# Activation buffers that begin 32 bytes apart within 256-byte lines, in a two-layer diffusion backbone

## The chip, the core and the metric

The kernel runs on one core of a Trainium2 chip. The metric is the device time of one execution in microseconds, from the core's first to its last instruction. A core has five engines with queues of their own: TensorE (PE in the rows; its weight loads are PEld), VectorE (DVE), ScalarE (ACT), GpSimd (POOL) and SyncE (SP, which here only starts transfers). Operands lie in SBUF, where each of 128 partitions has its own row of bytes; a buffer takes the same byte range in all of them. Products are summed in PSUM.

## The reference

Two layers over 512 latent tokens and 256 context tokens of 1024 features, in float32. All matrices are read from HBM in each run.

```python
for i in range(2):
    hc = modulate(cx, norm1_gain[i], mod_c[0], mod_c[1])      # RMSNorm, scale and shift
    zc = hc @ w_in[i]                                         # the last layer: keys and values alone
    hx = modulate(x, norm1_gain[i], mod_x[0], mod_x[1])
    zx = hx @ w_in[i]                                         # 1024 -> 5376
    attn_x = window_attention_with_context(qx, kx, vx, kc, vc, attn_sink[i])
    x = x + mod_x[2] * mixer_merge(zx, attn_x, *layer)        # pool, attention, spatial gating
    x = x + mod_x[5] * swiglu(modulate(x, ...), w_ffn_in[i], w_ffn_out[i])   # 1024 -> 2 x 2816 -> 1024
    # in the first layer the context goes the same way with its own attention
return rmsnorm(x, final_gain)
```

Here `mixer_merge` is `(sum over three branches of sigmoid(gate) * (y_branch @ w_br)) @ w_out`.

## The kernel before, in words

The stream of tokens is kept feature-major: features in the partitions, tokens along the row. `X` holds the residual. A large product takes a 128x128 block of a weight as the stationary operand and 512 columns (latents, `x` in a name) or 256 columns (context, `c`) of an activation tile as the moving one.

Every float32 product is made as three float32r products. `split_unit` (L272, L273) splits a weight into a high part `wh` and a low part `wl`; `split_act` (L318, L319) does the same with activations, into H and L. `gemm_step` then issues, per 128 features, wh with H (L290), wl with H (L291) and wh with L (L292). All of the gate, branch, output, query, key, value and FFN products go through it: 3 x 3112 instructions.

What stands where in SBUF: pools give out buffers of one size in turn, and the pools stand one behind the other:

- `cst`: constants, `X`, and the keys `KK` (moving operand of the scores, L505 and L511). The two tiles of `KK` begin 64 bytes into a 256-byte line.
- `rawp` (4 buffers of 4096 bytes) takes the loads of weights, and `hlp` (6 of 4096 bytes) their high and low parts. All ten begin 96 bytes into a line.
- `act` (11 buffers of 8192 bytes): high and low activations, queries, gate sums, the FFN's hidden tiles `fa`, the loaded tokens and the first modulation weights. 8192 is 32 x 256, so all eleven begin at the same place, 96 bytes into a line. A product's moving operand is a piece of such a buffer; the pieces are 1024 or 2048 bytes long and begin at multiples of 1024 bytes from the buffer's start.
- `tmp` (8 buffers of 2112 bytes), `att`, `macp` and `sml` follow. Since 2112 is 8 x 256 + 64, the buffers of `tmp` begin at 96, 160, 224 and 32 in turn.

Two lines carry this in the code:

```python
act = ctx.enter_context(tc.tile_pool(name="act", bufs=11))       # L56
hold = act.tile([P, 2 if two else 1, 2, TT], F32R, tag="S8", name=f"fa{l}{j}")   # one of its users, in ffn
```

The order of the instructions on every engine is the order in which the program is written; `Filler` mixes the vector work, a step at a time, with the large products. Nothing in that depends on an address.

Of the kernel before, what the change touches and what calls it, by code (L numbers as in the profile page):

```python
# [18 lines left out]
P = 128  # L19
# [16 lines left out]
class Stream:  # L36
    """Columns [t0, t0 + T) of the feature-major residual: the context or the latents."""

# [10 lines left out]
def hybrid_dit_kernel(ctx, tc, I, out):  # L49
# [5 lines left out]
    hlp = ctx.enter_context(tc.tile_pool(name="hlp", bufs=3))  # L55
    act = ctx.enter_context(tc.tile_pool(name="act", bufs=11))  # L56
    tmp = ctx.enter_context(tc.tile_pool(name="tmp", bufs=8))
# [17 lines left out]

# [1 line left out]
    ident = cst.tile([P, P], F32, name="ident")  # L77
# [14 lines left out]

    # rows of 128 features each, transposed to one column per row
    rowsA = t2("rowsA", P)[:48, :]
# [49 lines left out]
    def to_features(s):  # L144
        """The stream's residual to feature-major, and its tokens' sums of squares."""
        for b in range(s.t0 // P, s.t0 // P + s.NB):
            junk = act.tile([P, D], F32, tag="S8", name=f"junk{b}")
            S.activation(junk, xin[b], AF.Square, accum_out=ssx[:, b:b + 1])
            for k4 in range(2):
                ps = pmain(f"ps_xt{b}_{k4}")  # L150
                for k in range(4):
                    T_.transpose(ps[:, k * P:(k + 1) * P], xin[b][:, (k4 * 4 + k) * P:(k4 * 4 + k + 1) * P], ident)
                x = X[:, k4 * 4:k4 * 4 + 4, b * P:(b + 1) * P]
                if s is SC and k4:
                    S.activation(x, ps.rearrange("p (k t) -> p k t", k=4), AF.Copy)
                else:
                    V.tensor_copy(x, ps.rearrange("p (k t) -> p k t", k=4))
                yield

# [1 line left out]
    modv, A1, A2 = {}, {}, {}  # L161
# [10 lines left out]
    def take_mod(l, t0, n, ps, nv):  # L172
        """Rows of 32 features each to columns: tiles t0 .. t0 + n of the layer's modulation vectors."""
        mT = t2(f"mT{l}{t0}", n * 32)
        V.transpose(mT, ps)
        V.tensor_tensor(modv[l][:, t0:t0 + n, 0:nv], mT.rearrange("p (t c) -> p t c", c=32)[:, :, 0:nv],
                        colsB[:, l * 48 + t0:l * 48 + t0 + n].unsqueeze(2).to_broadcast([P, n, nv]), ALU.add)
        for dst, o, rg in ((A1[l], 8, R_N1), (A2[l], 32, R_N2)):
            a, b = max(o, t0), min(o + 8, t0 + n)
            if a < b:  # L180
                V.scalar_tensor_tensor(dst[:, a - o:b - o, 0:nv], modv[l][:, a:b, 0:nv], 1.0,
                                       colsA[:, rg + l * 8 + a - o:rg + l * 8 + b - o].unsqueeze(2).to_broadcast([P, b - a, nv]),
                                       ALU.add, ALU.mult)

    def mod_part(ps, h):
        """A quarter of the first layer's first shift and scale, on the tensor engine: loads, then two k-tiles at each step."""
        src = I["w_mod"][0, :, 0:2 * D].rearrange("(k p) (s n) -> p k s n", p=P, s=2)[:, :, :, h * 256:(h + 1) * 256]
# [16 lines left out]
    def mod_steps(l, u0, u1, stride=1):  # L204
        """The others, 512 at a time: weighted rows added up on the vector engines, then over the partitions."""
        for u in range(u0, u1):
# [35 lines left out]
    class Filler:  # L242
        """Work that is interleaved, a step at a time, with the large products."""

# [21 lines left out]

# [1 line left out]
    def split_unit(raw_ap, kt, n, nm, eng=None):  # L268
        """float32r high part and exact low part of a [P, kt, n] block of weights."""
        wh = hlp.tile([P, kt, n], F32R, tag="WH", name=f"wh_{nm}")  # L270
        wl = hlp.tile([P, kt, n], F32R, tag="WL", name=f"wl_{nm}")
        S.activation(wh, raw_ap, AF.Copy)  # L272
        (eng or V).tensor_tensor(wl, raw_ap, wh.bitcast(F32), ALU.subtract)  # L273
        return wh, wl

    def units(src, kt, nm, engs=()):
        """src [kt*P, n] -> per n-tile (wh, wl) as [P, kt, 128] views, loaded 4 KB a partition at a time."""
        n = src.shape[1]
# [18 lines left out]
    def gemms(pw, kt, H, L):  # L297
        """Products of several feature tiles with the same activations, side by side."""
        for k in range(kt):
            for ps, (wh, wl) in pw:  # L300
                gemm_step(ps, wh[:, k, :], wl[:, k, :], H[k], L[k], k == 0, k == kt - 1)

    def pair_tiles(n, T, nm):
        """n feature tiles of T columns, as high and low parts."""
        per = 2048 // T
# [17 lines left out]

# [1 line left out]
    def rstd(ss_ap, nb, nm, div):  # L325
# [6 lines left out]
    def token_ss(s, acc, nm):  # L332
        """Sums over the features of the squares that the tiles of acc hold."""
        ps = pmain(f"ps_ss_{nm}")
# [5 lines left out]
    def modulated(s, ss, A, Sh, nm, out, every=1, keep=False, HL=None):  # L340
        """Normed and modulated stream, split: the sums, the tokens' factors along the columns, the products."""
        rs = rstd(ss(), s.NB, nm, D)
# [30 lines left out]

# [1 line left out]
    KK = [cst.tile([P, 2, NT], F32R, name=f"KK{g}") for g in range(2)]  # L375
# [42 lines left out]
    def queries(s, l, H, L, rot, us, ts):  # L418
        """Rotated queries of the head pairs ts: a head's high parts in its half of the partitions, its low parts in the other."""
        Q = act.tile([P, len(ts), 2, s.T], F32R, tag="S8", name=f"Q{l}{s.name}{ts[0]}")  # L420
# [18 lines left out]
    def attention(s, l, H, L, rot, YH, YL, then=None):  # L439
        """A head pair and block of queries at each step, in a pipeline of three stages."""  # L440
        us = units(I["w_in"][l][:, OFF_Q:OFF_K], KT, f"q{l}{s.name}")
# [11 lines left out]
        def advance(w):  # L453
            """Transposes of the pair before the last and sums of the one before that; then new scores."""
            done.append(None)
# [33 lines left out]
    def score(s, l, w, Q):  # L489
        """Softmax of a head pair's scores, queries in the partitions."""  # L490
        t, b = w
# [34 lines left out]
    def turn(s, st):  # L526
        """The pair's weights with the keys in the partitions."""
        w, blocks, prs, nm = st
# [30 lines left out]
    def first_tiles(parts, e):  # L559
        """The context's first six feature tiles by quarters of the features: sv's four and two of u.  # L560

        A quarter of the modulation vectors is loaded and summed during the products of the one before."""
        cols = ((OFF_SV, 512), (OFF_U, 256))
# [112 lines left out]
    def pooling(s, l, H, L, YH, YL):  # L676
        """A pool group at each step."""
        nm0 = f"{l}{s.name}"
# [154 lines left out]
    def ffn(streams, l, hs, finish, starts=(), mods=(), parts=None, ahead=None, turn=None):  # L833
        """The up and down halves are a tile apart; starts are steps of what the last stream waits for."""
        fo = I["w_ffn_out"][l]
# [37 lines left out]
        def half(s, w, j, up, more=(), by=None):  # L873
            """Gate or up products of one stream, and of further tiles side by side."""
            pw = [(pmain(f"pf{'gu'[u]}{l}{s.name}{jj}")[:, :s.T], ww, jj, u) for ww, jj, u in ((w, j, up), *more)]
# [66 lines left out]

# [1 line left out]
    hs = {}  # L944
# [70 lines left out]
    def last_tiles(one, acc):  # L1015
        """The last products by token halves: a half is normed during the other's."""
        hs["x"] = pair_tiles(KT, SEQ, "n2x1")
# [18 lines left out]
    def first_halves(pw, H, L):  # L1036
        """The first products by token halves: the second half is normed during the first's."""
        for i in range(2):
# [17 lines left out]
    def turn(i):  # L1056
        """Residual rows to token-major, and the last gate's vector along the columns."""
        if i == 0:
# [12 lines left out]
    def finish1(c0, m, A):  # L1071
        """The last products with the tokens in the partitions; a block of tokens is normed and stored during the next."""
        ws = []
# [52 lines left out]
def _shape_constants():  # L1126
    """Rotation tables by grid position and the pools' edge factors: by shapes alone."""
    import numpy as np
# [36 lines left out]
```

## Time and profile before

| | |
|---|---|
| time, median of 2 runs | 2089.8 us (2088.78 to 2090.81) |
| profiled execution, span | 2093.8 us (no other time of it is given) |
| mean granted TensorE clock | 0.988 of full |
| TensorE busy | 2024.5 us, 97% of the span, 11615 matmuls |
| VectorE, ScalarE, GpSimd busy | 55%, 36%, 20% |
| DMA | 233.46 MB, 112 GB/s over the span |

Busy times come from one execution under the profiler. A matmul's duration holds its way through the array and overlaps the next one's, so the pace of a stream of matmuls is read from one start to the next, not from the duration.

### The profile page before, as it was taken

How to read it: one execution, taken by the hardware profiler on the slowest of the kernel's cores; microseconds unless marked ns; L12 is line 12 of the kernel's file. 1: busy time of each engine (PE TensorE's matmuls, PEld its weight loads, DVE VectorE, ACT ScalarE, POOL GpSimd, SP SyncE). 2: the span in 40 equal slices, each digit the busy share in tenths (PEclk: the TensorE clock that was granted, in tenths of full speed). 3: DMA queues.
4: the chain of work that ended last, by engine and by line, in shares of the span. 5: the costliest groups of instructions: out<-in, count | busy, mean ns of one | idle time of the engine just before them, and what ended most of it. 6: DMA issues, size and time to landing. Idle time of an engine off the chain costs nothing.

```text
span 2093.8 us, 28850 instructions
## 1 busy us (share of the span) xinstructions
PE 2024.5 (97%) x11615; PEld 1715.0 (82%) x11615; DVE 1149.6 (55%) x1765; ACT 744.4 (36%) x1231; POOL 426.7 (20%) x358
## 2 busy tenths in 40 slices
PE   7998999999899999999999999999999999999998
PEld 6988988777677888888888888787778788888887
DVE  4878638675666653434334335765756664344335
ACT  3655434344333422121313124443422333222223
POOL 4426302023664411000102013301111130000000
PEclk9999999999999999999999999999999999999999
DMA  9755633231544232222323223423336643333331
GB/s 294 207 165 153 202 101 101 63 104 51 159 153 131 81 91 73 88 81 71 91 61 101 71 71 89 109 61 90 88 102 211 178 132 91 100 95 97 101 92 59
DMA packets 326181, 233.46 MB, mean 112 GB/s; under 512 B 7648, under 2 KB 299664, under 8 KB 326048
## 3 DMA queue, kind: packets, MB, share of 16 engines
q1 hardware_dynamic: 322528, 226.78, 36.1%
q0 software_dynamic: 3280, 4.76, 1.1%
q8 instruction: 91, 1.49, 0.3%
q14 instruction: 42, 0.34, 0.0%
q10 hardware_dynamic: 240, 0.08, 0.0%
HBM read 225.30 MB, written 2.10 MB: 109 GB/s over the span
## 4 chain that ended last, share of the span: by engine, by line
PE 81%; DVE 10%; DMA 3%; issue 2%; ACT 2%; POOL 2%; ACTq 0%; SPq 0%; POOLq 0%; DVEq 0%
PE pg1x L290 2%; PE pg1x L291 2%; PE pg1x L292 2%; PE pfg0x L292 2%; PE pfg0x L291 2%; PE pfg0x L290 2%; PE pfg1x L292 2%; PE pfo0x L290 2%; PE pfo0x L291 2%; PE pfu1x L291 2%; PE pfo0x L292 2%; PE pfu1x L292 2%; PE pfu1x L290 2%; PE pfg1x L290 2%; PE pfg1x L291 2%
## 5 line engine op out<-in xcount | busy, mean ns | idle before, releaser
L220 POOL TENSOR_TENSOR mac<-mac,mq 128x512 f32<-128x512 f32 x84 | 124.4, 1481 | 296.9 <-ACT mq L219 293.0
L273 DVE TENSOR_TENSOR wl_fu<-raw_fu,wh_fu 128x1024 fp32r<-128x1024 f32 x44 | 63.6, 1446 | 153.9 <-ACT wh_fu L272 153.8
L222 DVE SCALAR_TENSOR_TENSOR mac<-wm,scv,mac 128x512 f32<-128x512 f32 x140 | 131.0, 936 | 13.4 <-DMA wm<-in_w_mod_dram 10.6
L272 ACT ACTIVATE wh_fg<-raw_fg 128x1024 fp32r<-128x1024 f32 x44 | 46.6, 1059 | 181.1 <-PE pfo0x L292 65.7
L273 DVE TENSOR_TENSOR wl_fo<-raw_fo,wh_fo 128x1024 fp32r<-128x1024 f32 x42 | 54.7, 1303 | 69.3 <-ACT wh_fo L272 69.3
L272 ACT ACTIVATE wh_fo<-raw_fo 128x1024 fp32r<-128x1024 f32 x42 | 44.4, 1058 | 122.4 <-issue 120.2
L291 PE MATMUL pg0x<-n1x0h,wl_g0x 128*128 128x512 f32 x192 | 77.2, 402 | 8.9 <-DVE wl_g0x L273 8.9
L290 PE MATMUL pg0x<-n1x0h,wh_g0x 128*128 128x512 f32 x192 | 77.1, 402 | 1.5 <-ACT wh_g0x L272 1.5
L290 PE MATMUL pg1x<-n1x1h,wh_g1x 128*128 128x512 f32 x192 | 76.4, 398 | 0.0
L292 PE MATMUL pg0x<-n1x0l,wh_g0x 128*128 128x512 f32 x192 | 76.4, 398 | 0.0
L291 PE MATMUL pg1x<-n1x1h,wl_g1x 128*128 128x512 f32 x192 | 75.8, 395 | 0.0
L292 PE MATMUL pg1x<-n1x1l,wh_g1x 128*128 128x512 f32 x192 | 75.8, 395 | 0.0
L329 POOL TENSOR_TENSOR rs_fin<-v_fin,half_neg 128x1 f32<-128x1 f32 x4 | 2.9, 721 | 355.3 <-DVE v_fin L327 355.3
L290 PE MATMUL pfg1x<-n2x1h,wh_fg 128*128 128x512 f32 (+1 forms) x184 | 70.5, 383 | 0.8 <-ACT n2x1h L359 0.8
L854 DVE SCALAR_TENSOR_TENSOR X<-pfo0x,modv,X 128x512 f32<-128x512 f32 x48 | 36.0, 750 | 64.0 <-PE pfo0x L292 64.0
L292 PE MATMUL pfg1x<-n2x1l,wh_fg 128*128 128x512 f32 (+1 forms) x184 | 70.5, 383 | 0.5 <-POOL n2x1l L360 0.3
L290 PE MATMUL pfu1x<-n2x1h,wh_fu 128*128 128x512 f32 (+1 forms) x184 | 70.0, 380 | 0.0
L291 PE MATMUL pfu1x<-n2x1h,wl_fu 128*128 128x512 f32 (+1 forms) x184 | 70.0, 380 | 0.0
L291 PE MATMUL pfg1x<-n2x1h,wl_fg 128*128 128x512 f32 (+1 forms) x184 | 69.9, 380 | 0.0
L292 PE MATMUL pfu1x<-n2x1l,wh_fu 128*128 128x512 f32 (+1 forms) x184 | 69.9, 380 | 0.0
L290 PE MATMUL pfo0x<-fa,wh_fo 128*128 128x512 f32 x176 | 69.0, 392 | 0.0
L291 PE MATMUL pfo0x<-fa,wl_fo 128*128 128x512 f32 x176 | 69.0, 392 | 0.0
(708 smaller groups left out, 6540.1 us busy)
## 6 DMA issues: line engine op xcount, KB each, us to landing
wm<-in_w_mod_dram SPq DMA_DIRECT2D x96, 512.0 KB, 4.0
raw_fg<-in_w_ffn_in_dram SPq DMA_DIRECT2D x44, 512.0 KB, 3.9
raw_fu<-in_w_ffn_in_dram SPq DMA_DIRECT2D x44, 512.0 KB, 3.8
raw_fo<-in_w_ffn_out_dram SPq DMA_DIRECT2D x42, 512.0 KB, 3.4
raw_g0c<-in_w_in_dram SPq DMA_DIRECT2D x24, 512.0 KB, 3.9
raw_g0x<-in_w_in_dram SPq DMA_DIRECT2D x24, 512.0 KB, 4.2
raw_g1x<-in_w_in_dram SPq DMA_DIRECT2D x24, 512.0 KB, 3.9
raw_wo0c<-in_w_out_dram SPq DMA_DIRECT2D x8, 512.0 KB, 4.0
```

Of the source, the lines that this page charges most:

```text
L220: G.tensor_tensor(a, a, q, ALU.add)
L222: V.scalar_tensor_tensor(a, raw[:, k, :], sck, a, ALU.mult, ALU.add)
L272: S.activation(wh, raw_ap, AF.Copy)
L273: (eng or V).tensor_tensor(wl, raw_ap, wh.bitcast(F32), ALU.subtract)
L290: T_.matmul(ps, wh, H, start=first, stop=False)
L291: T_.matmul(ps, wl, H, start=False, stop=False)
L292: T_.matmul(ps, wh, L, start=False, stop=last)
L329: G.tensor_tensor(rs, v, half_neg[:, :nb], ALU.pow)
L854: V.scalar_tensor_tensor(x, ps, modv[l][:, 40 + n, s.r:s.r + 1], x, ALU.mult, ALU.add)
```

## The change

The buffers of `act` grow from 8192 to 8224 bytes (2056 float32 numbers), and each tile uses the first bytes of its buffer as before. 8224 is 32 x 257, so buffer number b of the eleven begins at 96 + 32b, counted within 256 bytes: 96, 128, 160, 192, 224, 0, 32, 64, 96, 128, 160. The pools behind `act` move back by 11 x 32 = 352 bytes; those ahead of it (`cst`, `rawp`, `hlp`) stay. A class with a method `tile` stands in for the pool. Docstrings and comments are dropped as well. On each engine the same instructions stand in the same order with the same waits as before, and each tile has the buffer number it had.

```diff
-    act = ctx.enter_context(tc.tile_pool(name="act", bufs=11))
+    actp = ctx.enter_context(tc.tile_pool(name="act", bufs=11))
+
+    class Staggered:
+        @staticmethod
+        def tile(shape, dt, tag, name):
+            n = math.prod(shape[1:])
+            t = actp.tile([P, 2048 + 8], dt, tag=tag, name=name)[:, :n]
+            if len(shape) == 2:
+                return t
+            d = "abc"[:len(shape) - 1]
+            return t.rearrange(f"p ({' '.join(d)}) -> p {' '.join(d)}", **dict(zip(d[:-1], shape[1:-1])))
+
+    act = Staggered
```

By the places of its buffers, the program's 9336 products of L290 to L292 have moving operands that begin here:

| bytes into a 256-byte line | 0 | 32 | 64 | 96 | 128 | 160 | 192 | 224 |
|---|---|---|---|---|---|---|---|---|
| before, 512 columns | 0 | 0 | 0 | 5976 | 0 | 0 | 0 | 0 |
| before, 256 columns | 0 | 0 | 0 | 3360 | 0 | 0 | 0 | 0 |
| now, 512 columns | 856 | 296 | 864 | 1136 | 708 | 1184 | 260 | 672 |
| now, 256 columns | 16 | 176 | 224 | 168 | 296 | 1176 | 488 | 816 |

## Rows read from the trace of the kernel before

**Rows 1.** The page: span, and busy time of each engine.

```profile
span 2093.8 us, 28850 instructions
PE 2024.5 (97%) x11615; PEld 1715.0 (82%) x11615; DVE 1149.6 (55%) x1765; ACT 744.4 (36%) x1231; POOL 426.7 (20%) x358
```

**Rows 2.** The page: the chain that ended last, shares by engine.

```profile
PE 81%; DVE 10%; DMA 3%; issue 2%; ACT 2%; POOL 2%; ACTq 0%; SPq 0%; POOLq 0%; DVEq 0%
```

**Rows 3.** L290 over the span: busy us of its matmuls, then of their weight loads.

```profile
0.00:2093.80 2093.80, 1109.12 (x3112) 592.85 (x3112) 0.99 0.38 112
```

**Rows 4.** Timeline, TensorE, second half of an FFN block: start us, duration us, what.

```profile
854.43 0.28 PE L290 MATMUL pfo0c<-fa,wh_fo 128*128 128x256 f32 x1
...
855.39 0.28 PE L292 MATMUL pfo0c<-fa,wh_fo 128*128 128x256 f32 x1
855.51 0.40 PE L290 MATMUL pfo0x<-fa,wh_fo 128*128 128x512 f32 x1
855.74 0.40 PE L291 MATMUL pfo0x<-fa,wl_fo 128*128 128x512 f32 x1
855.98 0.39 PE L292 MATMUL pfo0x<-fa,wh_fo 128*128 128x512 f32 x1
...
856.67 0.39 PE L292 MATMUL pfo0x<-fa,wh_fo 128*128 128x512 f32 x1
...
858.26 0.28 PE L290 MATMUL pfo0c<-fa,wh_fo 128*128 128x256 f32 x1
```

**Rows 5.** Two stretches: busy us of PE, PEld, DVE, ACT, POOL, then granted clock.

```profile
562.70:565.70 3.00, 3.00 (x9) 2.32 (x8) 0.00 (x0) 0.00 (x0) 2.92 (x3) 0.50 0.78 237
856.60:858.30 1.70, 1.70 (x10) 1.38 (x9) 1.25 (x2) 0.00 (x0) 0.00 (x0) 1.00 0.00 0
```

**Rows 6.** Timeline, TensorE, in the first of these stretches.

```profile
563.12 0.63 PE L290 MATMUL pg0x<-n1x0h,wh_g0x 128*128 128x512 f32 x1
...
565.68 0.63 PE L290 MATMUL pg0x<-n1x0h,wh_g0x 128*128 128x512 f32 x1
```

**Rows 7.** Timeline, TensorE: scores, whose moving operand is KK.

```profile
81.98 0.28 PE L292 MATMUL pg0c<-n1c0l,wh_g0c 128*128 128x256 f32 x1
82.10 0.64 PE L511 MATMUL s0c<-KK,Q0c 128*128 128x256 f32 x4
82.57 0.28 PE L290 MATMUL pg0c<-n1c0h,wh_g0c 128*128 128x256 f32 x1
```

**Rows 8.** Timeline, TensorE: transposes, whose stationary operand is pr (96) or X (224).

```profile
97.96 0.60 PE L536 MATMUL pt0c<-ident,pr0c 128*128 128x128 f32 x4
2072.93 1.91 PE L1067 MATMUL ps_yt<-ident,X 128*128 128x128 f32 x16
```

**Rows 9.** Lines with durations, min/median/max in ns: operands in tmp's buffers.

```profile
L886 DVE TENSOR_TENSOR sg1x<-sg1x,pfu1x x22: 686/689/690, 1733.0 to 2073.1; 128x512 f32<-128x512 f32 x22
L883 ACT ACTIVATE sg1x<-pfg1x x22: 597/600/601, 1732.3 to 2064.5; 128x512 f32<-128x512 f32 x22
```

**Rows 10.** Groups of TensorE by line: busy us, mean ns of one.

```profile
L290 PE MATMUL pg0x<-n1x0h,wh_g0x 128*128 128x512 f32 x192 | 77.1, 402 | 1.5 <-ACT wh_g0x L272 1.5
L290 PE MATMUL pg1x<-n1x1h,wh_g1x 128*128 128x512 f32 x192 | 76.4, 398 | 0.0
L290 PE MATMUL pfu0x<-n2x0h,wh_fu 128*128 128x512 f32 x176 | 68.5, 389 | 0.0
```

**Rows 11.** DMA issues that write to or read from act's buffers: KB each, us to landing.

```profile
xin_c<-in_ctx_dram SPq DMA_DIRECT2D x1, 1024.0 KB, 4.9
Q0x<-ql0x POOLq DMA_DIRECT2D x8, 128.0 KB, 2.4
out_dram<-yt SPq DMA_DIRECT2D x4, 512.0 KB, 2.7
```

## The prediction

> **What bounds the kernel now.** I read the page's busy times first: TensorE works 97% of a span of 2093.8 us, and no other engine over 55% [rows 1]. The chain of waits agrees: 81% of what ended last is TensorE, 10% VectorE [rows 2]. The change alters no instruction, order or wait; it alters only where eleven buffers begin. So the question is one of duration: does any instruction take a different time when its operand begins elsewhere, and does it lie on TensorE's stream?
>
> Next I read the pace of that stream. Within a run of FFN products the start column goes from 854.43 to 855.51 over nine products of 256 columns: 0.120 us each. It goes from 856.67 to 858.26 over seven products of 512 columns: 0.227 us each [rows 4], at the full granted clock, 2.4 GHz [rows 5]. One column per cycle would be 256 / 2.4 = 106.7 ns and 512 / 2.4 = 213.3 ns. Both widths thus carry the **same excess of about 13.3 ns per product**. At the half level, 1.2 GHz [rows 5], the starts go from 563.12 to 565.68 over six products [rows 6]: 427 ns, which is 512 / 1.2 with no excess. The excess is therefore not so many cycles of the array; it looks like a fixed piece of time in fetching operands that a slower array hides.
>
> In the products of L290 to L292 (3 x 3112 [rows 3]) the excess adds up to 9336 x 13.3 ns = 124.5 us, 6% of the span. All of them read a moving operand that begins 96 bytes into a line. **This is the only sum of note that the change could touch**, and 13.3 ns is also the time in which 32 float32 columns, 128 bytes, stream in: the excess can be a fixed start of each product, or one more 128-byte step because 96 is not a multiple of 128. The rows of before contain no product that begins at 0 or 128, so they don't decide it.
>
> **The change part by part.**
>
> *Moving operands of the 9336 products.* The nearest row with another start is the scores: KK begins at 64. Four products of 256 columns follow a steady stream of the same width, and their starts go from 82.10 to 82.57: 117.5 ns each against 120 [rows 7]. So moving the start by 32 bytes was worth at most 2.5 ns there, and the excess stayed at 10.8 of 13.3. The four are few, and starts shift by a few ns where streams of different kinds meet: the first products behind a change of width take 0.23 and 0.24 us instead of 0.227 [rows 4]. I read the 2.5 ns as that. My value is 0 ns per product, by the nearest row; the ends are -13.3 ns (all of the excess gone) and +13.3 ns (one more such piece).
>
> *Stationary operands.* wh and wl stay at 96. Queries (288 score products) and the last 48 products have their stationary operand in `act`; if each gained or lost 13.3 ns that would be 336 x 13.3 = 4.5 us. Transposes show stationary operands at two places: four of pr (96) last 0.60 us together and sixteen of X (224) 1.91 us [rows 8]. Taking off one full duration of about 0.28 us, that is 0.32 / 3 = 107 ns and 1.63 / 15 = 109 ns: the same. I take 0.
>
> *VectorE, ScalarE, GpSimd.* They read and write `act`, and `tmp` moves by 352 bytes. The buffers of `tmp` already begin at four different places, and the 22 additions of L886 that go round them last 686 to 690 ns, the 22 activations of L883 597 to 601 ns [rows 9]. A start that differs by 32 bytes or a multiple changes at most 4 ns here. Few of these are on the chain (14% for the three engines [rows 2]), and I take 0.
>
> *Contention between engines.* If TensorE's reads collided with the others' accesses, products beside busy engines would be slower. The slowest large group, pg0x, has a mean of 402 ns against 389 in the undisturbed pfu0x; pg1x has 398 [rows 10]. Over three lines of 192 that is at most 13 x 576 + 9 x 576 ns = 12.7 us, waits and changes of stream included. This is the whole of what neighbours could cost now, so it bounds a gain at -12.7 us, and by the same size a loss. I take 0.
>
> *Transfers.* Loads of weights go to `rawp`, which stays. Into and out of `act` go the tokens, the first modulation weights, the queries' low parts and the result; such transfers land in 2.4 to 4.9 us [rows 11]. They began off a 256-byte line before and mostly do now. If each row of 4096 bytes took one 256-byte piece more or less than its 16, the last store would move by 2.7 / 16 = 0.2 us and the first load by 4.9 / 16 = 0.3 us. I take 0.
>
> The sum is 0: 2093.8 us for the profiled execution. That execution is 4.0 us above the median of the runs shown, so in their terms 2089.8 us.
>
> **A rule beside the row.** The Trainium skill, in "TensorE: Matmul & The Clock Gate", section "Back-to-back issue gap", gives a full-clock gap of N / 2.4 + 2.5 ns, 215.8 ns for 512 columns. This trace shows 227 [rows 4], so 10.8 ns per product are unexplained by it; were they all due to the buffers' places and gone, 9336 x 10.8 ns = 101 us would go, to 1989 us. The skill's "SBUF — State Buffer", section "Specifications", speaks against this: it names 16-byte lines, and every start here is a multiple of 32, which by that rule costs the same anywhere. No run here shows the size of a line.
>
> **The rivals.**
>
> 1. *Only multiples of 128 are free.* The excess is a seventeenth (ninth) 128-byte step. Then the products from buffers 1, 5 and 9 lose it: 856 + 708 = 1564 of 512 columns x 13.3 ns = 20.9 us, and 16 + 296 = 312 of 256 columns, where the 109 ns pace of the weight loads [rows 8] stops them at a gain of 11 ns: 3.4 us. Together -24 us, 2065 us, faster by 1.2%. For it speaks the exact size of the excess, and KK at 64 keeping most of it. If it falls smoothly instead by the 2.5 ns per 32 bytes of rows 7 within 128 bytes, the table's counts give a mean change of -3.7 ns (512) and -3.2 ns (256), -33 us, 2057 us.
>
> 2. *The gain is large.* Either multiples of 64 are free (2688 x 13.3 + 1024 x 11 ns = 47 us, 2043 us), or the excess comes from both operands beginning at the same place, 96, which now holds for only 1136 + 168 products: 4840 x 13.3 + 3192 x 11 ns = 99 us, 1990 us. Against both stand the scores: KK begins at 64 and its stationary Q at 96, and 10.8 ns of excess are left [rows 7].
>
> 3. *Slower: the upper half of a line costs one more step.* If a fetch works in lines of 256 bytes in halves, a moving operand that begins at 160, 192 or 224 takes a further 13.3 ns. That is 2116 + 2480 = 4596 products, +61 us, 2151 us, slower by 2.9%. It decides (over 2%, 42 us) from 9.1 ns per such product. No product of before begins in an upper half, so no moving operand excludes it; against it speak X at 224 as a stationary operand, which loads at the pace of pr [rows 8], and the other engines' indifference [rows 9]. A milder form has the excess grow by the 2.5 ns per 32 bytes of rows 7 over the whole line: the mean start goes from 96 to 109 (512) and 160 (256), +1.05 x 5976 + 5.0 x 3360 ns = +23 us, 2113 us.
>
> 4. *The change doesn't do what it says.* The sizes leave no room for this: the pool steps by 8224 bytes, a multiple of 32, and nothing else in it is shared with another tile. It would give the forecast's time in any case.
>
> **How the numbers follow.** The forecast, no effect of the place, has 0.59; rival 1 has 0.16, rival 2 0.10, rival 3 0.09, its milder form 0.06. The likeliest time is 2089.8 us; contention and stationary reads alone would leave it within 2073 to 2107. The range reaches to rival 1's smooth end and to the mild loss, 2056 to 2114 us, and holds 0.59 + 0.16 + 0.06 = 0.81. A difference of 2%, 42 us, is about what a measurement of this kernel can tell from no change. Faster by more is rival 2, 0.10; slower by more is rival 3, 0.09; the rest, 0.81, lies within.
>
> **What would show it.** In the changed kernel the start-to-start pace of steady runs settles it: 0.227 and 0.120 us in every run of FFN products proves the forecast, whatever buffer `fa`, n2x0h or n1x1h lies in. Rival 1 would show some runs at 0.213 to 0.216 and the rest at 0.227; since L290 and L291 read the high part and L292 the low one, a run could alternate between two paces. Rival 2 shows the fast pace in half or more of the runs, rival 3 a pace of 0.240 (512) and 0.133 (256) in buffers 2, 3, 4 and 10. L886 and L883 should stay at 689 and 600 ns. I am wrong if any steady run has a pace that differs from before by more than 2 ns.

## The result, and the profile after

| | before | after |
|---|---|---|
| time, median of 2 runs | 2089.8 us (2088.78 to 2090.81) | 2106.93 us (2106.62 to 2107.23) |
| ratio to before, 95% interval | | 1.008 (1.0051 to 1.011) |
| profiled execution: span, mean granted clock | 2093.8 us, 0.988 | 2104.4 us, 0.992 |

The change costs 17.1 us, 0.8%. That lies within 2% and within the range of the forecast, but it is not the forecast "no effect": the interval excludes a ratio of 1.

The page of the changed kernel: span, busy times, and the shares of the chain that ended last.

```profile
span 2104.4 us, 28850 instructions
PE 2033.8 (97%) x11615; PEld 1702.9 (81%) x11615; DVE 1148.0 (55%) x1765; ACT 744.0 (35%) x1231; POOL 429.4 (20%) x358
...
PE 82%; DVE 9%; DMA 3%; issue 2%; ACT 2%; POOL 1%; ACTq 0%; POOLq 0%; SPq 0%; DVEq 0%
```

Beside [rows 1, 2] TensorE's matmuls are busy for 9.3 us longer; the chain's shares agree to a point, and no new wait stands in it. Next, a stretch near the end in which TensorE never idles and no context is left, so that nearly all products have 512 columns: first before, then after (columns as in [rows 5]).

```profile
1800.00:2000.00 200.00, 200.00 (x884) 165.58 (x884) 77.68 (x85) 51.00 (x62) 0.00 (x0) 1.00 0.33 98
```

```profile
1800.00:2000.00 200.00, 200.00 (x866) 162.22 (x865) 77.33 (x84) 50.26 (x60) 0.00 (x0) 1.00 0.32 95
```

In the same 200 us at the full clock TensorE finishes 866 products instead of 884: 230.9 ns each instead of 226.2. The timeline of the changed kernel shows the pace itself (start us, duration us, what); lines 304 to 306 are L290 to L292 of before.

```profile
564.61 0.63 PE L304 MATMUL pg0x<-n1x0h,wh_g0x 128*128 128x512 f32 x1
...
565.89 0.63 PE L304 MATMUL pg0x<-n1x0h,wh_g0x 128*128 128x512 f32 x1
...
857.27 0.40 PE L304 MATMUL pfo0x<-fa,wh_fo 128*128 128x512 f32 x1
...
858.45 0.39 PE L306 MATMUL pfo0x<-fa,wh_fo 128*128 128x512 f32 x1
...
860.07 0.28 PE L304 MATMUL pfo0c<-fa,wh_fo 128*128 128x256 f32 x1
...
1006.17 0.28 PE L304 MATMUL pfu0c<-n2c0h,wh_fu 128*128 128x256 f32 x1
...
1008.98 0.39 PE L304 MATMUL pfg0x<-n2x0h,wh_fg 128*128 128x512 f32 x1
```

Twelve products of 512 columns take 2.80 us, 233 ns each. Twelve such products of before (from 855.51 to 858.26 in [rows 4]) take 2.75 us, 229 ns each. The last seven of each twelve (from 858.45 here, from 856.67 there) take 231 ns against 227. Twenty-four products of 256 columns take 2.81 us, 117 ns each, against 120. So the wide ones became slower and the narrow ones faster. At the half clock three products take 1.28 us, 427 ns, as in [rows 6]. Two of the runs below agree (426.7 ns at distance 32, 426.0 at 160): there the place does nothing.

Here and below, a mean pace is taken over all products that run at the full clock and are followed by one of the same width without a wait (some 5,700 of the 5976 and 3,100 of the 3360). It is 227.44 and 119.68 ns before, 231.45 and 117.88 ns after. 5976 x 4.01 - 3360 x 1.80 ns = **+17.9 us, as much as the whole loss**. The profiled spans differ by only 10.6 us because the execution of after met less of the half clock. Span times mean granted clock, as an estimate of the span at the full clock throughout, is 2067.9 us before and 2088.6 us after (mean clocks 0.98766 and 0.99249), 20.7 us apart.

### The profile page after: what moved, and what is told of

It is laid out like the page before. It is cut to its first block, busy times and chain, and to the rows that moved or that the text cites. A ratio compares the mean times of both kernels' runs of the same rounds, so it can differ in the third digit from the quotient of the medians.

```text
span 2104.4 us, 28850 instructions
## 1 busy us (share of the span) xinstructions
PE 2033.8 (97%) x11615; PEld 1702.9 (81%) x11615; DVE 1148.0 (55%) x1765; ACT 744.0 (35%) x1231; POOL 429.4 (20%) x358
## 3 DMA queue, kind: packets, MB, share of 16 engines
q1 hardware_dynamic: 322528, 226.78, 35.9%
## 4 chain that ended last, share of the span: by engine, by line
PE 82%; DVE 9%; DMA 3%; issue 2%; ACT 2%; POOL 1%; ACTq 0%; POOLq 0%; SPq 0%; DVEq 0%
PE pg1x L304 2%; PE pg1x L305 2%; PE pg1x L306 2%; PE pfg0x L306 2%; PE pfg1x L306 2%; PE pfg0x L305 2%; PE pfo0x L306 2%; PE pfu1x L305 2%; PE pfu1x L306 2%; PE pfo0x L305 2%; PE pfo0x L304 2%; PE pfg0x L304 2%; PE pfu1x L304 2%; PE pfg1x L305 2%; PE pfg1x L304 2%
## 5 line engine op out<-in xcount | busy, mean ns | idle before, releaser
L236 DVE SCALAR_TENSOR_TENSOR mac<-wm,scv,mac 128x512 f32<-128x512 f32 x140 | 129.3, 923 | 13.3 <-DMA wm<-in_w_mod_dram 10.7
L306 PE MATMUL pfg0x<-n2x0l,wh_fg 128*128 128x512 f32 x176 | 69.2, 393 | 0.3 <-POOL n2x0l L374 0.3
```

The costliest lines, as they stand in the source:

```text
L236: V.scalar_tensor_tensor(a, raw[:, k, :], sck, a, ALU.mult, ALU.add)
L306: T_.matmul(ps, wh, L, start=False, stop=last)
```

## The experiments

Three theories of why a moving operand's place changes the pace: **A**, its distance from the place of the stationary operand (wh or wl), both counted within 256 bytes, decides; **B**, jumps in place from one moving operand to the next cost time; **C**, its own place within a line decides (rivals 1 and 3 of the prediction).

### All buffers of `act` moved alike

The size stays 8192, so that no two moving operands differ in place, and a pad ahead of the pool moves all eleven buffers. With 8 numbers (32 bytes):

```diff
     hlp = ctx.enter_context(tc.tile_pool(name="hlp", bufs=3))
+    pad = ctx.enter_context(tc.tile_pool(name="pad", bufs=1))
+    V.memset(pad.tile([P, 8], F32, name="pad"), 0.0)
     act = ctx.enter_context(tc.tile_pool(name="act", bufs=11))
```

The others have 16, 24, 32, 40, 48, 56 and 64 numbers. `hlp` stays, so the distance from stationary to moving operand is the size of the pad. Expected, in the order in which they ran, for 32, 64 and 128 bytes:

> All eleven activation buffers begin at 128 instead of 96 (8192 bytes apart, as before); the weights' high and low parts stay at 96. Theory A (the place of the moving operand against the stationary one's, here 32 bytes apart, sets the pace): the steady paces leave 0.2267 and 0.120 us everywhere; if they go to the changed kernel's means of about 0.2315 and 0.118, the time rises by 5976 x 4.8 - 3360 x 2 ns = 22 us, to 2112 us. Theory B (a cost only where one product's moving operand begins elsewhere than the one's before): no change, 2090 us, 0.2267 and 0.120. Theory C (the absolute place, multiples of 128 free): 0.2133 in all runs, about 2090 - 117 = 1973 us.

> As the run by 32, with all activation buffers at 160, 64 bytes from the weights' 96. Theory A: paces of their own, neither those of before nor necessarily those of the shift by 32; a change of 10 us or more either way. Theory B: 2090 us, 0.2267 and 0.120. Theory C: 160 is 32 past a multiple of 128, so the excess stays: 2090 us.

> As the run by 32, with all activation buffers at 224, half a 256-byte line from the weights' 96. Theory A: the largest change of the three if the two reads meet in a period of 256 bytes, none if the period is 128 or less (2090 us then). Theory B: 2090 us. Theory C with the upper half costing more: 0.240 and 0.133 us, 2090 + 124 = 2214 us; with multiples of 128 alone: 2090 us.

Then for 96, 160, 192, 224 and, in a third group, 256 bytes:

> All activation buffers 96 bytes behind the weights' place (at 192). The first four runs left Theory A alone: the place against the weights sets the pace (0: 227.4 and 119.7 ns; 32: 233.3 and 116.9; 64: 229.1 and 116.7; 128: 232.9 and 118.8). Theory A1 (even multiples of 64 are cheap, odd ones of 32 dear, 128 the exception): as by 32, about 233 and 117 ns, 2114 us. Theory A2 (no pattern in 32s): anything from 227 to 235.

> All activation buffers 160 bytes behind the weights' place (at 0, a full 256-byte line's start). Theory A with a period of 128 bytes: as by 32, 233.3 and 116.9 ns, 2114 us; but the run by 128 differs from the one at 0, so a period of 256 is likelier. Theory C once more (the start of a 256-byte line is free): 0.2133 us, 1970 us; not expected after the run with the weights shifted too.

> All activation buffers 192 bytes behind the weights' place (at 32). Theory A with the cost even in the distance (192 is 64 ahead in a line of 256): as by 64, 229.1 and 116.7 ns, 2092 us. If it is not even, another value from 227 to 235 ns.

> All activation buffers 224 bytes behind, which is 32 ahead, of the weights' place (at 64). Theory A, even in the distance: as by 32, 233.3 and 116.9 ns, 2114 us. With these eight the changed kernel's time can be summed: its 512-column products by place against the weights 0, 32, ... 224 are 1136, 708, 1184, 260, 672, 856, 296, 864, its 256-column ones 168, 296, 1176, 488, 816, 16, 176, 224. If the places alone matter, the counts times these runs' paces give its 17 us; if switching between places costs too (Theory B), the sum falls short of it.

> All activation buffers 256 bytes further on, at 96 again. Theory A with a period of 256 bytes: as before, 227.4 and 119.7 ns, 2091 us. A longer period (512 or more): an eighth value of 229 to 234 ns for 512 columns, 2100 to 2120 us.

Measured (the fourth column is what the two paces make of 5976 and 3360 products, the fifth is against before on the same chip):

| distance, bytes | 512 columns, ns | 256 columns, ns | sum, us | measured, us | ratio, 95% interval |
|---|---|---|---|---|---|
| 0 (before) | 227.44 | 119.68 | | | |
| 32 | 233.30 | 116.95 | +25.8 | +22.5 | 1.0113 (1.0096 to 1.0129) |
| 64 | 229.07 | 116.65 | -0.4 | +0.6 | 1.001 (1.000 to 1.002) |
| 96 | 233.35 | 119.87 | +36.0 | +28.5 | 1.0145 (1.0128 to 1.0161) |
| 128 | 232.85 | 118.80 | +29.4 | +24.6 | 1.0123 (1.0107 to 1.0138) |
| 160 | 234.19 | 117.96 | +34.6 | +32.0 | 1.0156 (1.0141 to 1.0171) |
| 192 | 233.21 | 114.72 | +17.8 | +16.7 | 1.0089 (1.007 to 1.0108) |
| 224 | 233.25 | 118.46 | +30.6 | +25.0 | 1.0126 (1.0109 to 1.0143) |
| 256 | 227.45 | 119.69 | +0.1 | +1.0 | 1.0008 (0.9998 to 1.0017) |

The stretch from 1800 to 2000 us of distances 32, 64, 160 and 256, in this order:

```profile
1800.00:2000.00 200.00, 200.00 (x859) 160.92 (x858) 76.83 (x84) 49.74 (x60) 0.00 (x0) 1.00 0.31 94
```

```profile
1800.00:2000.00 200.00, 200.00 (x876) 164.09 (x875) 77.47 (x85) 50.27 (x60) 0.00 (x0) 1.00 0.32 96
```

```profile
1800.00:2000.00 200.00, 200.00 (x855) 160.80 (x854) 76.45 (x83) 49.18 (x59) 0.00 (x0) 1.00 0.31 93
```

```profile
1800.00:2000.00 200.00, 200.00 (x884) 165.62 (x883) 78.95 (x86) 51.84 (x62) 0.00 (x0) 1.00 0.33 98
```

859, 876, 855 and again 884 products: the pace comes back after 256 bytes. A period of 128 bytes is excluded by distance 128, which has 232.85 ns. Distance 64 shows that the time alone is a poor witness: its wide products lose 1.63 ns each, its narrow ones gain 3.03 ns, and the two cancel to +0.6 us. My narrower guesses within A failed: a change of 10 us at 64, one value for all odd multiples of 32 (256 columns take 116.95 ns at 32, 119.87 at 96), and a cost that is even in the distance (192 isn't like 64, and 224 is like 32 for 512 columns alone).

Since there are no jumps in these runs, B isn't needed for the effect. It adds nothing on average either: if each of the change's products ran at the mean pace of its distance (place minus 96, with the counts of the table in the section on the change), the means would be 231.42 and 117.84 ns; 231.45 and 117.88 were measured. Multiples of 128 aren't free: distance 160 begins at 0 of a line and is the slowest. The sums overstate most losses by a few us (7.5 at the most). Products at the half clock don't pay the slower pace; I take it that products that wait don't either, which no run shows by itself.

### The weights moved

With the pad of 8 numbers ahead of `rawp`, weights and activations both go from 96 to 128 (distance 0, another place). With 56 numbers ahead of `hlp` and 8 ahead of `act`, the activations are back at 96 and the weights lie at 64 (distance 32, the old place of the moving operand).

```diff
     cst = ctx.enter_context(tc.tile_pool(name="cst", bufs=1))
+    pad = ctx.enter_context(tc.tile_pool(name="pad", bufs=1))
+    V.memset(pad.tile([P, 8], F32, name="pad"), 0.0)
     rawp = ctx.enter_context(tc.tile_pool(name="rawp", bufs=4))
```

```diff
+    padh = ctx.enter_context(tc.tile_pool(name="padh", bufs=1))
+    V.memset(padh.tile([P, 56], F32, name="padh"), 0.0)
     hlp = ctx.enter_context(tc.tile_pool(name="hlp", bufs=3))
+    pada = ctx.enter_context(tc.tile_pool(name="pada", bufs=1))
+    V.memset(pada.tile([P, 8], F32, name="pada"), 0.0)
     act = ctx.enter_context(tc.tile_pool(name="act", bufs=11))
```

> Weights' loads, their high and low parts and the activation buffers all begin at 128 instead of 96: the place against each other is as before, the absolute place is not. Theory A: 2090 us, paces 0.2267 and 0.120. Theory B: 2090 us as well. Theory C (multiples of 128 free): about 1973 us, or whatever the run by 32 of the activations alone gives.

> The activation buffers stay where they are before (96); the high and low parts of the weights move to 64, so the moving operand is 32 behind the stationary one. Theory A (the two reads of TensorE, moving and stationary): as the run that moved the activations by 32 instead, 233.3 and 116.9 ns, about 2114 us. If the partner of the activations is another buffer (the loads at 96, keys, constants), or the partner is what other engines write: 2091 us.

The same stretch, first with both at 128, then with the weights alone at 64:

```profile
1800.00:2000.00 200.00, 200.00 (x884) 165.58 (x883) 79.89 (x87) 51.84 (x62) 0.00 (x0) 1.00 0.33 97
```

```profile
1800.00:2000.00 200.00, 200.00 (x859) 160.64 (x858) 76.10 (x83) 50.20 (x60) 0.00 (x0) 1.00 0.32 95
```

Both at 128: 2089.01 us, ratio 0.9992 (0.9982 to 1.0002), paces 227.40 and 119.65 ns, as before. Weights alone at 64: 2115.7 us, ratio 1.0126 (1.0109 to 1.0142), paces 233.29 and 116.94 ns, those of distance 32 within a hundredth. The moving operands lie where they lay before, and yet every product has the other pace. **This settles A against C**: it is the distance between the two operands.

### A layout by width

Distance 0 has the best mean for 512 columns, 192 for 256 columns. Two kernels give each width its own. In the first, the weights of context products keep their place and all others move by 192 bytes, as `act` does; `fa` has its context piece at 192 as well. FFN gate and up products share their weights between the streams and stay at 0. A few constants were merged to make room.

```diff
+    def halves_of(shape, nm):
+        o = 0 if "c" in nm or "first" in nm else 48
...
+        th = hlp.tile([P, 1088], F32R, tag="WH", name=f"wh_{nm}")
...
+        return [t[:, o:o + n].rearrange("p (k n) -> p k n", k=shape[1]) for t in (th, tl)]
```

> The place by width: 512-column products keep 0 bytes between their operands (227.4 ns), and 2064 of the 256-column ones get 192 (the weights' parts of the context's mixer begin 64 bytes past the activations' place, the context's part of the FFN's hidden tile 192 past it; the other 1296 stay at 0). Some small constants share space to make room. Theory A: 2064 x (119.7 - 114.7) ns = 10.2 us less, ratio 0.995. Theory B (switching between places costs): the hidden tiles alternate between places from product to product, and part of the gain is lost; ratio 0.996 or more.

Measured 2089.68 us, ratio 0.9994 (0.9984 to 1.0004): no gain that can be told. The paces did change: 2064 context products are at distance 192 and take 115.62 ns (8.4 us less), and the latents keep 227.3. The mean granted clock was 0.9883 over its eleven runs and 0.9904 over the twenty of before beside them; span times clock fell by 5.1 us (2068.0 to 2062.9, means), and the lower clock took 0.0021 x 2088 = 4.4 us back. Whether the layout or chance lowered the clock stays open, and so does what became of the rest of the 8.4 us.

The second moves only the FFN's context operands, all 1584, to distance 192:

```diff
+        if nm == "n2c0":
+            last = att.tile([P, 1280], F32R, tag="pT", bufs=1, name=f"{nm}last")
...
+                HL.append([t[:, 48 + i * T:48 + (i + 1) * T] for i in range(7)] + [last[:, 48 + x * T:48 + (x + 1) * T]])
...
-            o, a = 0, {}
+            o, a = 0 if len(streams) == 1 else 48, {}
```

> Only the context's tiles in the first layer's FFN are moved: their normed tiles and their part of the hidden tiles begin 192 bytes past the weights' place (1584 products of 256 columns); all else stays at 0. There TensorE waited only about 2 us on these products before, so a gain has no wait to turn into, unlike the context's mixer in the run by width. Theory A by the runs' paces: 1056 gate and up products x (119.9 - 114.0) ns = 6.2 us, and 528 output products, which change place every 12, x (119.3 - 117.5) ns = 1 us: -7 us, ratio 0.9966. If the gain is only moved into waits again, or into slower latents behind each change of place: ratio 0.999 to 1.000.

Measured **2085.6 us, ratio 0.997 (0.9958 to 0.9981)**, 5.6 us less than before and the fastest of all. The moved products give less than was hoped for: they take 117.26 ns, not the 114.0 that the same groups (gate, up and output of the context) had in the run with all at 192, so 1584 x 2.42 ns = 3.8 us.

The latents gave something too, although their own distance stays 0. The twelve output products that took 2.75 us in [rows 4] take 2.72 us behind context products at 192:

```profile
846.76 0.39 PE L290 MATMUL pfo0x<-fa,wh_fo 128*128 128x512 f32 x1
...
849.48 0.28 PE L290 MATMUL pfo0c<-fa,wh_fo 128*128 128x256 f32 x1
```

In the mean pfo0x went from 229.04 to 226.78 ns and pfg0x, which also follows the context, from 227.75 to 226.80; 528 products of each make 1.7 us. Together the paces give 5.5 us. Span times clock fell by 3.7 us only, and the mean granted clock was 0.9906 against 0.9894, which may be chance; how the 5.6 us divide between pace and clock isn't settled.

Why 117 and not 114? The gate and up products of one block (24 each) show it. Before, distance 0:

```profile
1003.72 0.28 PE L290 MATMUL pfu0c<-n2c0h,wh_fu 128*128 128x256 f32 x1
...
1006.60 0.40 PE L290 MATMUL pfg0x<-n2x0h,wh_fg 128*128 128x512 f32 x1
```

All at 192:

```profile
1002.57 0.28 PE L292 MATMUL pfu0c<-n2c0h,wh_fu 128*128 128x256 f32 x1
...
1005.29 0.39 PE L292 MATMUL pfg0x<-n2x0h,wh_fg 128*128 128x512 f32 x1
```

Only the FFN's context at 192, at two times:

```profile
828.44 0.51 PE L230 MATMUL ps_mod<-mac,pick 128*32 128x128 f32 x12
828.88 0.38 PE L290 MATMUL pfg0c<-n2c0h,wh_fg 128*128 128x256 f32 x1
...
829.46 0.28 PE L291 MATMUL pfg0c<-n2c0h,wl_fg 128*128 128x256 f32 x1
...
831.73 0.28 PE L290 MATMUL pfu0c<-n2c0h,wh_fu 128*128 128x256 f32 x1
...
834.45 0.39 PE L290 MATMUL pfg0x<-n2x0h,wh_fg 128*128 128x512 f32 x1
...
994.89 0.28 PE L290 MATMUL pfg0c<-n2c0h,wh_fg 128*128 128x256 f32 x1
...
997.72 0.28 PE L290 MATMUL pfu0c<-n2c0h,wh_fu 128*128 128x256 f32 x1
...
1000.55 0.39 PE L290 MATMUL pfg0x<-n2x0h,wh_fg 128*128 128x512 f32 x1
```

The 24 up products (pfu0c) take 2.88 us before (120 ns each), 2.72 with all at 192 (113), and in the last kernel 2.72 once and 2.83 (118) the other time, from the same tiles and at the same distance. So distance 192 has **two steady paces**, and once settled, each of these streams kept its own to the end. In the last kernel all 17 context gate streams that follow directly on latents' FFN products (distance 0) run at 118 ns. The three that follow `ps_mod` settle at 113 to 114 after their first four products: above, the other 20 take 2.27 us, from 829.46 to 831.73. With all at 192, 16 of the 17 that follow such latents (now at 192 too) run at 113 to 114, but the first of them at 118. So what stands ahead mostly goes with the pace that a stream has; that it alone decides isn't shown, and the first stream speaks against it. No theory foresaw this, and it is why the moved products gave 3.8 us here instead of the 9.0 us (1584 x 5.7 ns) that 114.0 ns would have given.

## Why the prediction was wrong, point by point

- **What bounds the kernel**: right. TensorE's stream sets the end, order and waits didn't change, and the pace of L290 to L292 accounts for the loss. (The 4.0 us between the profiled span and the median mix two measures: in the execution of after, the time is 2.2 us longer than the span.)
- **Moving operands of the 9336 products: the failed step.** I took 0 "by the nearest row", KK's 117.5 ns against 120 [rows 7], and read the 2.5 ns as starts that shift between streams. They fit the effect: KK lies 32 bytes ahead of Q (distance 224), where the full run has 118.46 ns. The row was also of the wrong width. It had 256 columns, on which most shifts gain; the 512 columns, which are 64% of the products and carry all of the loss, were never seen at a second distance. A term whose ends are ±13.3 ns and whose one witness is of another width should have kept most of the chance open. Measured: +4.01 and -1.80 ns.
- **The common excess of 13.3 ns**: it is not a fixed start of each product. Only at distance 0 is it nearly one value (227 or 226 ns for 86% of the 512s, 120 for 86% of the 256s); elsewhere 512 columns cost 229.07 to 234.19 ns in the mean. That it vanishes at the half clock was right.
- **Stationary operands**: their own place costs nothing, as taken (both at 128: 2089.01 us). Their place against the moving operand is the effect, and the sum had no term for that; only rival 2 named it.
- **Other engines, contention, transfers**: 0, as taken. Of the changed kernel:

```profile
L900 DVE TENSOR_TENSOR sg1x<-sg1x,pfu1x x22: 686/687/690, 1736.5 to 2083.7; 128x512 f32<-128x512 f32 x22
L897 ACT ACTIVATE sg1x<-pfg1x x22: 597/599/601, 1735.9 to 2075.0; 128x512 f32<-128x512 f32 x22
```

  These are L886 and L883 of [rows 9], within 2 ns in the median.
- **Rival 1** (multiples of 128 are free) and **rival 3** (upper half of a line): wrong, place alone decides nothing. Rival 3's mild form came nearest in time (2113 us), by a mechanism that isn't there; that the measured time lies within the range, whose upper end is this form's, is luck. **Rival 2's** second form named the right pair, both operands' places against each other, with the sign reversed: for 512 columns equal places are the best case, not the worst. I judged it by KK again, and rival 2 as a whole had 0.10. **Rival 4**: the buffers do lie where the table says, since the means that its counts give are the measured ones.
- **The sign that I named** ("a pace that differs from before by more than 2 ns") was met: 231 against 227 ns in the last seven of the twelve pfo0x.
- **What can be told apart**: 2%, 42 us, was far too coarse. The interval of after excludes 1 at 0.8%, and that of the last kernel at 0.3%.
- **The Trainium skill's figures**: the prediction's gap of 215.8 ns for 512 columns didn't come; no layout here brought their mean below 227.17 ns. From the 16-byte lines of the Trainium skill ("SBUF — State Buffer", section "Specifications") I took it that starts at multiples of 32 bytes cost the same. They don't here: whole multiples of 32 bytes changed the mean pace by up to 6.75 ns. The Trainium skill's "SBUF — State Buffer", section "Who interferes with whom", calls TensorE's two read ports (moving operand, weight load) independent. At the full clock the pace here wasn't independent of the two places: moving the weights alone by 32 bytes took 512 columns from 227.44 to 233.29 ns. Whether the ports themselves are the reason, no run shows.

## What to carry to other kernels

Where products stream back to back at the full clock, each with its own weight load, the place of the moving operand against the weights within 256 bytes was worth up to 3% of the pace for 512 columns and 4% for 256 here. For 512 columns it was best that the two begin alike; for 256 columns that was close to the worst. So find the best distance for the width that carries most of the time, and change the size of a buffer knowing that it shifts everything behind it. A row of another shape is no witness for a term: before taking 0, ask whether any row shows the decisive shape with the one thing changed. And read a small shift in a short stream as a possible effect until many products show that it is noise.

## What the runs showed of the hardware that I had not expected

- Products of float32r operands have a pace that depends on the distance between moving and stationary operand with a period of 256 bytes: 227.4 to 234.2 ns for 512 columns, 114.7 to 119.9 for 256, with the best distance at 0 for the first and at 192 for the second. At the half clock 512 columns take 426 to 427 ns at each distance at which I read it (0, 32, 96, 128, 160, 192).
- At one distance there can be two steady paces (113 and 118 ns for 256 columns at 192), and in most streams what runs ahead goes with the one or the other. A stream's mean pace also changed where its own distance stayed at 0 and the stream ahead of it was moved (pfg0x, 227.75 and 226.80 ns). The paces by distance are therefore means over this program's order.
- Why this is so, the runs don't show. It looks like weight loads and moving reads that meet in SBUF, but nothing here separates the two reads, and the other engines' writes into these buffers moved along with them. Steps under 32 bytes weren't tried either.
